# The written order of an MLP's instructions where one unit of columns hands over to the next

## Chip, cores, metric

The kernel runs on one core of a Trainium2 chip. The metric is device time in microseconds (us) of one execution; lower is better. The core has TensorE (PE, with its weight loads PEld), VectorE (DVE), ScalarE (ACT), GpSimd (POOL) and SyncE (SP), which here only issues loads. Each engine works through its own queue in order and waits at an instruction until what it needs is there.

## What is computed

Two decoder layers on 256 tokens of width 2048, in float32. Each layer attends (differential attention in layer 1, dilated windows in layer 2, both with four heads that read a memory), adds the result to the stream x, and ends with the MLP that the change is about:

```python
hm = _rmsnorm(x, g_mlp[i])
x = x + jnp.square(jax.nn.relu(hm @ w_mlp1[i])) @ w_mlp2[i]     # 2048 -> 8192 -> 2048
```

A last RMSNorm follows. In layer 2 the attention needs tables of key distances (`distances`), which are made from an iota.

## The kernel before

**Passes.** A float32 product is made of three fp32r matmuls: each operand is split into `hi` (a copy rounded by ACT) and `lo` (what is left, a subtraction on DVE), and `passes` (L609 to L612) adds hi x hi, hi x lo and lo x hi into one bank of PSUM. `split` (L116 to L118) is that pair of instructions, ACT first, then DVE.

**Units.** The 8192 hidden columns are cut into 8 units of 1024. Unit 0 goes up in the plain way (`up_plain`). Units 1 to 7 go up by a Strassen-like scheme: 8 steps (`step_up`), one for each pair of 128-row slices, each of 7 factors (p1 to p7) of 3 matmuls, 21 in all, which add up in 7 PSUM banks. `prep_up` makes the weights of one step in four parts: loads `b` and `o` (SP) and the sum `s` (DVE, L229); the split of `b` (`bh`, `bl`); `o` from `s` (L233), the split `oh`, a second sum (L235) and the split of `s`; the split of `o` (`th`, `tl`).

**The end of a unit.** `end_up` copies bank p1 (ACT L663), joins the banks on DVE (L666 to L674) into four 128x512 tiles c11, m12, c21 and m22, and squares them on ACT (L615, L616). `to_hT` turns each of these four **blocks** with four transposes on PE (L687) into a PSUM tile `pu` and splits it into `hT` (ACT L117, DVE L118). Blocks 0 and 1 are tokens 0 to 127, blocks 2 and 3 are tokens 128 to 255.

**Down.** Eight groups for each unit (`group_down`): 4 column groups n times 2 halves of tokens t, each of 24 matmuls into a bank `psd`, in the order of four weight pieces k = 0, 2, 4, 6 of two slices each. A piece is a load `raw_d`, a copy `hi_d` (ACT L698, `piece_hi`) and a subtraction `lo_d` (DVE L704, `piece_lo`). ACT then scales the bank into `part` (L723), and POOL issues a DMA that adds it to x (L724).

**Order.** Inside `tc.manual_schedule()` each engine gets its instructions in the order in which the code writes them; outside of it a planner orders them. The written loop runs over the units c and g = 0 to 7: one step of a later unit, then group g (n = g // 2, t = g % 2) of unit c. g = 0 to 6 hold the steps 1 to 7 of unit c + 1, g = 7 holds step 0 of unit c + 2, and `end_up(c + 1)` is written in g = 6 and g = 7. So PE takes 21 matmuls of a step, 24 of a group, and so on, and the weights of the next step and group are made beside them. There are 6 such **passages** from one unit to the next in each layer, 12 in all; the first unit and the last of a layer are written apart.

**Buffers.** PSUM has two tags of four banks: "m" (p1, p2, p5, p7) and "a" (p3, p6, p4 and one bank that `psd` and `pu` use in turn). `hi_d` and `lo_d` have 4 buffers each (WH), so the copy of the next n for piece k waits until PE has read the old piece k. `raw_d` has 3, with the fourth piece (k = 6) in the tag "ux" of `b` and `o` (5 buffers). The joined tiles, the sums of squares (`junk`) and `feat_sum` use the tag "ev" (4), the parts and the temporary tiles the tag "tmp" (6).

Of the kernel before, what the change touches and what calls it, by code (L numbers as in the profile page):

```python
# [17 lines left out]
P = 128  # L18
# [13 lines left out]
EV = 4  # L32
# [26 lines left out]
def trunk(ctx: ExitStack, tc: tile.TileContext, x, mem, g_attn, w_in, w_out, lambda_qk,  # L59
# [292 lines left out]

    def distances(groups, nm):

        dist_i = work.tile([P, 384], I32, tag="tmp", bufs=TMP, name=f"dist_i{nm}")
        nc.gpsimd.iota(dist_i[:, 0:128], pattern=[[-1, 128]], base=0, channel_multiplier=1)
        nc.gpsimd.iota(dist_i[:, 128:384], pattern=[[-1, 256]], base=128, channel_multiplier=1)
        tabs = []
        for gi, (window, dil) in enumerate(groups):
            if gi % 2 == 0:  # L360
                two = upool.tile([P, 2, 384], F32, tag="ut", bufs=UT, name=f"dist{nm}{gi}")
            tab = two[:, gi % 2, :]
            nc.vector.tensor_copy(tab, dist_i)
            keep_if(tab, 0, -1, 1)
            if dil > 1:
                rem_i = work.tile([P, 384], I32, tag="tmp", bufs=TMP, name=f"rem{nm}{gi}")
                nc.vector.tensor_scalar(rem_i, dist_i, dil - 1, None, op0=ALU.bitwise_and)
                rem = work.tile([P, 384], F32, tag="tmp", bufs=TMP, name=f"remf{nm}{gi}")
                nc.vector.tensor_copy(rem, rem_i)
                nc.vector.tensor_scalar(rem, rem, 1.0, FAR, op0=ALU.min, op1=ALU.mult)  # L370
                nc.vector.tensor_tensor(tab, tab, rem, op=ALU.max)
            if window < S:
                keep_if(tab, window, 1, -1)
            tabs.append(tab)
        return tabs
# [66 lines left out]
    for i in range(DEPTH):  # L442
# [156 lines left out]


        NC = DFF // 1024
        hT = [None, None]

        ublk = {}
        final = i == DEPTH - 1
# [52 lines left out]
        def end_up(c):  # L658
# [16 lines left out]
            ublk[c] = ((c11, 0, 0), (m12, 0, 1), (c21, 1, 0), (m22, 1, 1))  # L675
            yield
            squared(c21, c21, 1.0)
            squared(m22, m22, -1.0)

        def to_hT(c):  # L680

            for f in range(2):
                hT[f] = act_tile(f"hT{i}{c}{f}")
            for n, (u, t, f) in enumerate(ublk[c]):
                pt = bank([P, 4, P], f"pu_{i}{c}{n}")
                for k in range(4):
                    nc.tensor.transpose(pt[:, k], u[:, k * P:(k + 1) * P], ident)  # L687
                cols = slice(t * P, (t + 1) * P)
                split(hT[f][:, :, 0, cols], hT[f][:, :, 1, cols], pt)
                yield  # L690

        def piece_hi(c, n, k):
# [21 lines left out]
        def group_down(c, n, t, gemm):  # L714

            ps = bank([P, 512], f"psd{i}{c}{n}{t}", gemm)
            for k in range(8):
                passes(ps, hT[k // 4][:, k % 4, :, t * P:(t + 1) * P], *dw[c, n, k], k == 0, k == 7)
            return ps

        def add_down(c, n, t, ps):
# [33 lines left out]
        next(first)  # L755
        with tc.manual_schedule():
            run(prep_up(1, 0))
            run(first)
            prep = prep_up(1, 1)
            next(prep)  # L760
            step_up(1, 0)
            run(prep)
            piece_hi(0, 0, 0)
            piece_hi(0, 0, 2)
            piece_lo(0, 0, 0)
            turned = None
            for c in range(NC - 1):
                for g in range(8):
                    uc, kp = (c + 1, g + 1) if g < 7 else (c + 2, 0)
# [1 line left out]
                    prep = prep_up(pc, pk) if pc < NC else iter(())  # L771
                    n, t = g // 2, g % 2
                    more = (c, n + 1) if n < 3 else (c + 1, 0)
                    if g == 0:
                        turned = to_hT(c)

                        def turn_first():
                            next(turned)
                            piece_lo(c, 0, 2)
                            next(prep)  # L780

                        def turn_second():
                            next(turned)
                            next(prep)

                        step_up(uc, kp, {1: turn_first, 3: turn_second, 5: lambda: next(turned)})
                        prep_down(c, 0, (1,))
                        run(prep)
                    elif g == 1:
                        step_up(uc, kp, {2: lambda: run(turned)})  # L790
                        run(prep)
                    elif g == 6:
                        step_up(uc, kp)
# [1 line left out]
                        next(ending)  # L795
                        run(prep)
                        next(ending)
                    elif g == 7:
                        if uc < NC:
                            step_up(uc, kp)  # L800
                        for _ in range(3):
                            next(prep, None)
                        run(ending)
                        piece_hi(*more, 0)
                        run(prep)
                        piece_hi(*more, 2)
                        piece_lo(*more, 0)
                    else:
                        step_up(uc, kp)
                        run(prep)  # L810
                    if t == 1 and g < 7:
                        prep_down(*more, (0,))
                    add_down(c, n, t, group_down(c, n, t, False))
                    if t == 1 and g < 7:
                        prep_down(*more, (1,))
            piece_lo(NC - 1, 0, 2)
            prep_down(NC - 1, 0, (1,))
            run(to_hT(NC - 1))
        last_down(NC - 1)
        xT = nxt  # L820

# [9 lines left out]
    def add_last(t, c0, c1, acc):  # L831
# [3 lines left out]
        for f in range(2):  # L835
            for kk in range(4):
                hi, lo = wt[4 * f + kk]
                ah = hT[f][:, kk, 0, t * P:(t + 1) * P]
                al = hT[f][:, kk, 1, t * P:(t + 1) * P]
                for lhs, rhs in ((ah, hi), (ah, lo), (al, hi)):  # L840
                    nc.tensor.matmul(ps[:, c0:c1], lhs, rhs[:, c0:c1], start=n == 0, stop=n == 23)
                    n += 1
# [47 lines left out]
```

## Time and profile before

| | us |
|---|---|
| median of 3 runs | 2244.4 |
| lowest, highest | 2243.36, 2247.9 |
| the profiled execution, its own time | 2243.37 |
| its span in the profile | 2241.6 |
| one passage to the next in the written loop (the copy of piece 4 behind the `part` of g = 5: 583.57, 671.27, 759.01 us) | 87.7 |

TensorE's granted clock, as a share of its full speed, is 0.995 over the span. The MLPs stand at about 500 to 1180 us and 1560 to 2230 us. In the timeline a matmul of 512 columns shows 0.39 us, but one starts about every 0.23 us: they overlap, so lost time on PE is read from the distance of two starts, not from busy time.

### The profile page before, as it was taken

Reading aid. Unit: us, or ns where it says so; the run is one execution under the profiler, and the core shown is the slowest. Engines: PE = TensorE matmul, PEld = TensorE weight load, DVE = VectorE, ACT = ScalarE, POOL = GpSimd, SP = SyncE. Lnnn points to the kernel's source line nnn. Section 1 sums busy time; section 2 is a strip of 40 time slices with the busy share of each in tenths; the row PEclk is TensorE's granted clock in tenths of the full one; section 3 lists DMA queues with packets and bytes.
Section 4 is the critical chain, followed back from the end, with each engine's and each line's share of the span. In section 5 each row is a group of like instructions: output and inputs, shape, how many; then the busy total and the mean of one; then the engine's idle time right before and its main releaser. Section 6 shows DMA issues by size and latency. Waiting matters only on the chain.

```text
span 2241.6 us, 28416 instructions
## 1 busy us (share of the span) xinstructions
PE 2181.0 (97%) x10358; PEld 1794.2 (80%) x10358; DVE 1711.9 (76%) x2084; ACT 1326.3 (59%) x1840; POOL 115.7 (5%) x146
## 2 busy tenths in 40 slices
PE   9999999999999999999999999999999999999998
PEld 7888878887787787877878888888778778777786
DVE  6557766767889888988866665665888989888875
ACT  7445555556666666666655554455666666666664
POOL 0000000000000000000010000000000000000000
PEclk9999999999999999999999999999999999999999
DMA  7665556566677776776745556666677777777674
GB/s 247 189 194 162 152 169 197 170 194 195 203 234 212 205 235 195 228 223 199 215 138 188 160 171 181 194 187 197 193 209 233 206 209 225 207 212 233 195 211 145
DMA packets 262399, 443.50 MB, mean 198 GB/s; under 512 B 14497, under 2 KB 80242, under 8 KB 262002
## 3 DMA queue, kind: packets, MB, share of 16 engines
q1 hardware_dynamic: 245856, 412.14, 58.7%
q0 software_dynamic: 16128, 29.37, 7.3%
q8 instruction: 81, 1.33, 0.2%
q14 instruction: 60, 0.49, 0.1%
q10 hardware_dynamic: 274, 0.17, 0.0%
HBM read 409.12 MB, written 3.15 MB: 184 GB/s over the span
## 4 chain that ended last, share of the span: by engine, by line
PE 81%; ACT 7%; DVE 7%; issue 3%; DMA 1%; ACTq 0%; DVEq 0%; SPq 0%; POOL 0%; POOLq 0%
PE psd L610 8%; PE psd L612 8%; PE psd L611 8%; PE p L610 6%; PE p L611 5%; PE p L612 5%; PE ps_k L145 4%; PE ps_q L145 4%; PE pso L166 2%; PE pso L167 2%; PE pso L165 2%; PE ps_q L141 2%; PE ps_k L141 2%; PE psv L165 2%; PE psv L166 2%
## 5 line engine op out<-in xcount | busy, mean ns | idle before, releaser
L610 PE MATMUL psd<-hi_d,hT 128*128 128x512 f32 x1008 | 394.5, 392 | 3.6 <-ACT hT L117 3.3
L612 PE MATMUL psd<-hi_d,hT 128*128 128x512 f32 x1008 | 392.7, 390 | 2.8 <-DVE hT L118 2.8
L611 PE MATMUL psd<-lo_d,hT 128*128 128x512 f32 x1008 | 392.9, 390 | 0.0
L704 DVE TENSOR_TENSOR lo_d<-raw_d,hi_d 128x1024 fp32r<-128x1024 f32 x252 | 299.1, 1222 | 83.9 <-ACT hi_d L698 83.9
L698 ACT ACTIVATE hi_d<-raw_d 128x1024 fp32r<-128x1024 f32 x252 | 256.5, 1050 | 14.3 <-PE psd L612 8.1
L610 PEld LDWEIGHTS psd<-hi_d,hT 128*128 128x128 f32 x1008 | 189.5, 188 | 49.5 <-DVE hT L118 5.9
L612 PEld LDWEIGHTS psd<-hi_d,hT 128*128 128x128 f32 x1008 | 189.7, 188 | 42.9 <-DVE hT L118 3.6
L117 ACT ACTIVATE th<-o 128x1024 fp32r<-128x1024 f32 x112 | 118.8, 1061 | 174.9 <-DVE o L235 174.1
L611 PEld LDWEIGHTS psd<-lo_d,hT 128*128 128x128 f32 x1008 | 189.8, 188 | 38.8
L118 DVE TENSOR_TENSOR bl<-b,bh 128x1024 fp32r<-128x1024 f32 x112 | 136.5, 1219 | 40.9 <-ACT bh L117 40.9
L724 POOL DMA_DIRECT2D x_sb<-part x112 | 97.5, 871 | 1219.2 <-ACT part L723 1219.2
L117 ACT ACTIVATE sh<-s 128x1024 fp32r<-128x1024 f32 x112 | 118.7, 1060 | 63.7 <-DVE s L229 50.7
L118 DVE TENSOR_TENSOR tl<-o,th 128x1024 fp32r<-128x1024 f32 x112 | 137.3, 1226 | 22.1 <-ACT th L117 16.7
L229 DVE TENSOR_TENSOR s<-b,o 128x1024 f32<-128x1024 f32 x112 | 136.4, 1218 | 4.9 <-DMA o<-in_w_mlp_dram 4.9
L118 DVE TENSOR_TENSOR sl<-s,sh 128x1024 fp32r<-128x1024 f32 x112 | 136.3, 1217 | 0.0
L117 ACT ACTIVATE bh<-b 128x1024 fp32r<-128x1024 f32 x112 | 118.0, 1053 | 13.1 <-PE p L611 12.4
L723 ACT ACTIVATE part<-psd,rsq 128x512 f32<-128x512 f32 x112 | 76.8, 686 | 80.8 <-PE psd L612 79.2
L145 PE MATMUL ps_k<-xT,hi_k 128*128 128x512 f32 x384 | 122.3, 398 | 0.0
L145 PE MATMUL ps_q<-xT,hi_q 128*128 128x512 f32 x384 | 122.0, 399 | 0.0
L118 DVE TENSOR_TENSOR lo_v<-raw_v,hi_v 128x1024 fp32r<-128x1024 f32 x48 | 58.8, 1225 | 50.2 <-ACT hi_v L117 50.1
L610 PE MATMUL p<-bh,cb_xm 128*128 128x512 f32 x224 | 89.7, 400 | 3.9 <-DVE u L670 3.9
L610 PE MATMUL p<-sh,cb_xm 128*128 128x512 f32 x224 | 89.8, 401 | 0.0
(331 smaller groups left out, 4890.8 us busy)
## 6 DMA issues: line engine op xcount, KB each, us to landing
raw_d<-in_w_mlp_dram SPq DMA_DIRECT2D x252, 512.0 KB, 5.8
b<-in_w_mlp_dram SPq DMA_DIRECT2D x112, 512.0 KB, 3.9
o<-in_w_mlp_dram SPq DMA_DIRECT2D x112, 512.0 KB, 3.8
x_sb<-part POOLq DMA_DIRECT2D x112, 256.0 KB, 5.9
raw_q<-in_w_in_dram SPq DMA_DIRECT2D x48, 512.0 KB, 3.8
raw_k<-in_w_in_dram SPq DMA_DIRECT2D x48, 512.0 KB, 3.9
raw_v<-in_w_in_dram SPq DMA_DIRECT2D x48, 512.0 KB, 3.6
raw_o<-in_w_out_dram SPq DMA_DIRECT2D x48, 512.0 KB, 3.7
```

Of the source, the lines that this page charges most:

```text
L117: nc.scalar.activation(dst_hi, src, AF.Copy)
L118: nc.vector.tensor_tensor(dst_lo, src, dst_hi.bitcast(F32), op=ALU.subtract)
L141: nc.tensor.matmul(ps[j][:, 0, :], lo[:, j * P:(j + 1) * P], a[:, 0, :], **f)
L145: nc.tensor.matmul(ps[j].rearrange("p h t -> p (h t)"), hi[:, j * P:(j + 1) * P], a.rearrange("p h t -> p (h t)"), **f)
L165: nc.tensor.matmul(ps[t], ah, hi, start=first and kk == 0, stop=False)
L229: nc.vector.tensor_tensor(s, b, o[:, 0:1].to_broadcast([P, 2, 512]), op=ALU.add)
L610: nc.tensor.matmul(ps, acts[:, 0, :], hi, start=first, stop=False)
L611: nc.tensor.matmul(ps, acts[:, 0, :], lo, start=False, stop=False)
L612: nc.tensor.matmul(ps, acts[:, 1, :], hi, start=False, stop=last)
L698: nc.scalar.activation(hi, raw, AF.Copy)
L704: nc.vector.tensor_tensor(lo, raw, hi.bitcast(F32), op=ALU.subtract)
L724: nc.gpsimd.dma_start(x_sb[:, t, n * 512:(n + 1) * 512], part, accum_op=ALU.add)
```

## The change

- In a passage (g = 0 with c > 0) only blocks 0 and 1 are turned, ahead of the factors at places 2 and 4 of the step; blocks 2 and 3 are turned in the same way in g = 1. Before, three blocks were turned in g = 0 (ahead of places 1, 3 and 5) and one in g = 1.
- The squares of c21 and m22 move from g = 7 into g = 0, between and behind the first two blocks (`ending`).
- At g = 7 the four parts of `prep_up` run without a break; then the copy and the subtraction of piece 0, the group, and only behind the group's `part` the copy of piece 2, whose subtraction is the first of g = 0.
- At g = 1, 3 and 5 the copy of piece 4 is written ahead of the group and of its `part`; behind it come the copy of piece 6 and then the two subtractions.
- First unit: its pieces 0 and 2 are made ahead of the squares of unit 0, and blocks 0 and 1 are turned in step 0 of unit 1 (places 2 and 5), 2 and 3 in g = 1. Before, all four were turned in steps 1 and 2.
- Last unit: blocks 0 and 1 are turned ahead of group g = 7 of the unit before, 2 and 3 behind it; before, all four behind it.
- `dist_i`, the iota from which the distance tables are made, moves from the tag "tmp" to the tag "ev".

```diff
@@ -352,7 +352,7 @@
 
     def distances(groups, nm):
 
-        dist_i = work.tile([P, 384], I32, tag="tmp", bufs=TMP, name=f"dist_i{nm}")
+        dist_i = work.tile([P, 384], I32, tag="ev", bufs=EV, name=f"dist_i{nm}")
         nc.gpsimd.iota(dist_i[:, 0:128], pattern=[[-1, 128]], base=0, channel_multiplier=1)
         nc.gpsimd.iota(dist_i[:, 128:384], pattern=[[-1, 256]], base=128, channel_multiplier=1)
...
@@ -675,18 +675,19 @@
             ublk[c] = ((c11, 0, 0), (m12, 0, 1), (c21, 1, 0), (m22, 1, 1))
             yield
             squared(c21, c21, 1.0)
+            yield
             squared(m22, m22, -1.0)
 
         def to_hT(c):
 
             for f in range(2):
-                hT[f] = act_tile(f"hT{i}{c}{f}")
+                hT[c, f] = act_tile(f"hT{i}{c}{f}")
             for n, (u, t, f) in enumerate(ublk[c]):
                 pt = bank([P, 4, P], f"pu_{i}{c}{n}")
                 for k in range(4):
                     nc.tensor.transpose(pt[:, k], u[:, k * P:(k + 1) * P], ident)
                 cols = slice(t * P, (t + 1) * P)
-                split(hT[f][:, :, 0, cols], hT[f][:, :, 1, cols], pt)
+                split(hT[c, f][:, :, 0, cols], hT[c, f][:, :, 1, cols], pt)
                 yield
 
...
@@ -755,15 +756,12 @@
         next(first)
         with tc.manual_schedule():
             run(prep_up(1, 0))
+            prep_down(0, 0, (0,))
             run(first)
+            turned = to_hT(0)
             prep = prep_up(1, 1)
-            next(prep)
-            step_up(1, 0)
+            step_up(1, 0, {2: lambda: (next(turned), next(prep)), 5: lambda: next(turned)})
             run(prep)
-            piece_hi(0, 0, 0)
-            piece_hi(0, 0, 2)
-            piece_lo(0, 0, 0)
-            turned = None
             for c in range(NC - 1):
                 for g in range(8):
                     uc, kp = (c + 1, g + 1) if g < 7 else (c + 2, 0)
@@ -771,23 +769,29 @@
                     prep = prep_up(pc, pk) if pc < NC else iter(())
                     n, t = g // 2, g % 2
                     more = (c, n + 1) if n < 3 else (c + 1, 0)
-                    if g == 0:
-                        turned = to_hT(c)
-
+                    if g == 0 and c:
                         def turn_first():
                             next(turned)
-                            piece_lo(c, 0, 2)
+                            next(ending)
                             next(prep)
 
                         def turn_second():
                             next(turned)
                             next(prep)
 
-                        step_up(uc, kp, {1: turn_first, 3: turn_second, 5: lambda: next(turned)})
+                        turned = to_hT(c)
+                        piece_lo(c, 0, 2)
+                        step_up(uc, kp, {2: turn_first, 4: turn_second})
+                        prep_down(c, 0, (1,))
+                        next(prep)
+                        run(ending)
+                        run(prep)
+                    elif g == 0:
+                        step_up(uc, kp)
                         prep_down(c, 0, (1,))
                         run(prep)
                     elif g == 1:
-                        step_up(uc, kp, {2: lambda: run(turned)})
+                        step_up(uc, kp, {2: lambda: (next(turned), next(prep)), 4: lambda: run(turned)})
                         run(prep)
                     elif g == 6:
                         step_up(uc, kp)
@@ -795,27 +799,34 @@
                         next(ending)
                         run(prep)
                         next(ending)
+                    elif g == 7 and uc < NC:
+                        step_up(uc, kp)
+                        run(prep)
+                        piece_hi(*more, 0)
+                        piece_lo(*more, 0)
                     elif g == 7:
-                        if uc < NC:
-                            step_up(uc, kp)
-                        for _ in range(3):
-                            next(prep, None)
                         run(ending)
+                        turned = to_hT(c + 1)
+                        next(turned)
+                        next(turned)
                         piece_hi(*more, 0)
-                        run(prep)
-                        piece_hi(*more, 2)
                         piece_lo(*more, 0)
                     else:
                         step_up(uc, kp)
                         run(prep)
                     if t == 1 and g < 7:
                         prep_down(*more, (0,))
+                        piece_hi(*more, 4)
                     add_down(c, n, t, group_down(c, n, t, False))
                     if t == 1 and g < 7:
-                        prep_down(*more, (1,))
+                        piece_hi(*more, 6)
+                        piece_lo(*more, 4)
+                        piece_lo(*more, 6)
+                    elif t == 1:
+                        piece_hi(*more, 2)
+            run(turned)
             piece_lo(NC - 1, 0, 2)
             prep_down(NC - 1, 0, (1,))
-            run(to_hT(NC - 1))
         last_down(NC - 1)
         xT = nxt
```

The other lines rename `hT[f]` to `hT[c, f]`. The number of matmuls, transposes, splits and loads is the same.

## Rows read from the trace of the kernel before

**Rows 1.** The page, part 1: busy time, share of the span and instructions of each engine.

```profile
PE 2181.0 (97%) x10358; PEld 1794.2 (80%) x10358; DVE 1711.9 (76%) x2084; ACT 1326.3 (59%) x1840; POOL 115.7 (5%) x146
```

**Rows 2.** Who PE waited for over the whole span: engine, tile and line that waited, who ended the wait, us in total, times, longest us.

```profile
PE pu L687 <- DVE hT L118: 16.7, 14, 3.4
PE pu L687 <- ACT part L723: 11.3, 12, 1.0
PE p L610 <- DVE u L666: 6.6, 12, 0.6
PE p L610 <- DVE u L670: 3.9, 12, 0.3
PE psd L612 <- DVE hT L118: 2.8, 1, 2.8
```

**Rows 3.** Timeline of PE, the step of g = 7 in one passage of layer 2: start, duration, line, operation, tiles, and in brackets the idle time before it and who ended it.

```profile
1652.53 0.39 PE L610 MATMUL p<-bh,cb_xm 128*128 128x512 f32 x1
...
1653.91 0.47 PE L610 MATMUL p<-oh,cb_xm 128*128 128x512 f32 x1 [0.55 <-DVE u L666]
...
1655.87 0.50 PE L610 MATMUL p<-bh,cb_xm 128*128 128x512 f32 x1 [0.32 <-DVE u L670]
```

**Rows 4.** The same timeline, the step of g = 0 with three turned blocks, up to the first matmul of its group.

```profile
1664.19 0.39 PE L610 MATMUL p<-bh,cb_xm 128*128 128x512 f32 x1
...
1665.97 0.66 PE L687 MATMUL pu<-ident,u 128*128 128x128 f32 x4 [0.94 <-ACT part L723]
1666.38 0.47 PE L610 MATMUL p<-bh,cb_xm 128*128 128x512 f32 x1
...
1668.04 0.66 PE L687 MATMUL pu<-ident,u 128*128 128x128 f32 x4
...
1670.91 0.66 PE L687 MATMUL pu<-ident,u 128*128 128x128 f32 x4 [0.82 <-DVE hT L118]
...
1672.98 0.50 PE L610 MATMUL psd<-hi_d,hT 128*128 128x512 f32 x1
```

**Rows 5.** The same timeline, the step of g = 1 with one turned block, up to the first matmul of its group.

```profile
1678.55 0.39 PE L610 MATMUL p<-bh,cb_xm 128*128 128x512 f32 x1
...
1679.92 0.60 PE L687 MATMUL pu<-ident,u 128*128 128x128 f32 x4
...
1683.81 0.39 PE L610 MATMUL psd<-hi_d,hT 128*128 128x512 f32 x1
```

**Rows 6.** Timeline of DVE from the weights of g = 5 to the joining of the banks (x2 is two instructions in a row).

```profile
1640.04 2.35 DVE L704 TENSOR_TENSOR lo_d<-raw_d,hi_d 128x1024 fp32r<-128x1024 f32 x2
1644.20 2.36 DVE L704 TENSOR_TENSOR lo_d<-raw_d,hi_d 128x1024 fp32r<-128x1024 f32 x2 [1.80 <-ACT hi_d L698]
...
1653.09 0.68 DVE L666 TENSOR_TENSOR u<-t,p 128x512 f32<-128x512 f32 x1
...
1655.12 0.69 DVE L670 TENSOR_TENSOR u<-t,p 128x512 f32<-128x512 f32 x1
```

**Rows 7.** Timeline of ACT: the copies around the `part` of g = 5, and the `part` of g = 7.

```profile
1638.77 2.10 ACT L698 ACTIVATE hi_d<-raw_d 128x1024 fp32r<-128x1024 f32 x2
1642.53 0.69 ACT L723 ACTIVATE part<-psd,rsq 128x512 f32<-128x512 f32 x1 [1.65 <-PE psd L612]
1643.11 2.00 ACT L698 ACTIVATE hi_d<-raw_d 128x1024 fp32r<-128x1024 f32 x2
...
1665.25 0.67 ACT L723 ACTIVATE part<-psd,rsq 128x512 f32<-128x512 f32 x1
```

**Rows 8.** Timeline at the first unit of layer 2: PE from the start of its step 0, through the second turned block, to the first matmul of its first group, and DVE's first split of the weights of step 1.

```profile
1569.42 0.39 PE L612 MATMUL p<-bh,cb_xm 128*128 128x512 f32 x1
...
1579.80 0.92 PE L687 MATMUL pu<-ident,u 128*128 128x128 f32 x4 [3.39 <-DVE hT L118]
...
1585.28 0.50 PE L610 MATMUL psd<-hi_d,hT 128*128 128x512 f32 x1
...
1572.33 1.23 DVE L118 TENSOR_TENSOR bl<-b,bh 128x1024 fp32r<-128x1024 f32 x1 [11.44 <-ACT bh L117]
```

**Rows 9.** Timeline at the last unit: PE in layer 1 (all 16 transposes, then the 14th matmul of the next group), PE in layer 2 (the transposes, then the 8th matmul), and a weight subtraction of DVE in layer 1; then two stretches with length, busy time of PE, PEld, DVE, ACT and POOL (and instructions), PE's granted clock, share of DMA and GB/s.

```profile
1124.70 1.91 PE L687 MATMUL pu<-ident,u 128*128 128x128 f32 x16
...
1136.48 0.40 PE L612 MATMUL psd<-hi_d,hT 128*128 128x512 f32 x1
...
2184.26 1.91 PE L687 MATMUL pu<-ident,u 128*128 128x128 f32 x16
...
2189.95 0.39 PE L612 MATMUL psd<-hi_d,hT 128*128 128x512 f32 x1
...
1127.15 1.66 DVE L704 TENSOR_TENSOR lo_d<-raw_d,hi_d 128x1024 fp32r<-128x1024 f32 x1
...
1128.00:1137.00 9.00, 5.95 (x16) 4.08 (x17) 8.17 (x13) 1.43 (x3) 2.59 (x6) 0.62 0.49 142
2184.00:2194.00 10.00, 8.35 (x43) 6.45 (x42) 6.17 (x8) 4.53 (x7) 0.86 (x1) 1.00 0.74 212
```

**Rows 10.** The loads of the weight pieces over the whole span (KB each, median us from issue to landing), SP's issue of the pieces 0 and 2 for the passage shown above, and who reads the distance tables (times; duration min/median/max in ns; first and last start in us).

```profile
raw_d<-in_w_mlp_dram SPq DMA_DIRECT2D x252, 512.0 KB, 5.8
...
1641.28 1.50 SPq L85 DMA_DIRECT2D raw_d<-in_w_mlp_dram  x2
...
L425 DVE SCALAR_TENSOR_TENSOR e<-dist,sc x36: 545/548/555, 182.9 to 1372.7; 128x384 f32<-128x384 f32 x36
```

More of the change, by code (lines that the diff above doesn't have):

```diff
@@ L601, in trunk @@
         NC = DFF // 1024
-        hT = [None, None]
+        hT = {}
         ublk = {}
@@ L717, in group_down @@
             for k in range(8):
-                passes(ps, hT[k // 4][:, k % 4, :, t * P:(t + 1) * P], *dw[c, n, k], k == 0, k == 7)
+                passes(ps, hT[c, k // 4][:, k % 4, :, t * P:(t + 1) * P], *dw[c, n, k], k == 0, k == 7)
             return ps
@@ L837, in add_last @@
                 hi, lo = wt[4 * f + kk]
-                ah = hT[f][:, kk, 0, t * P:(t + 1) * P]
-                al = hT[f][:, kk, 1, t * P:(t + 1) * P]
+                ah = hT[NC - 1, f][:, kk, 0, t * P:(t + 1) * P]
+                al = hT[NC - 1, f][:, kk, 1, t * P:(t + 1) * P]
                 for lhs, rhs in ((ah, hi), (ah, lo), (al, hi)):
```

## The prediction

> **What bounds the kernel now.** I read busy time first: PE is in work for 2181.0 of 2241.6 us, DVE for 1711.9, ACT for 1326.3 [rows 1]. So only what PE loses can be won. Next, whom PE waited for [rows 2]: four lines come 12 times or more, as often as there are passages. A wait of 0.55 us ends with L666 and one of 0.33 with L670 (6.6/12, 3.9/12), one of 0.94 with a `part` (11.3/12), and 0.82 with an `hT` split (of its 14 times two are 3.39 us long, the rest is about 0.82). Last the timeline of one passage [rows 3 to 5]. From 1655.87 to 1664.19 are 12 matmuls of the step and 24 of the group; less 0.1 us for a slow restart that is 0.228 us each. From 1652.53 to 1683.81, three steps and two groups, are 31.28 us; 111 matmuls at 0.228 are 25.31. A passage thus loses 6.0 us: 1.4 at the two bank waits of g = 7 (1653.91 is 0.70 behind 1652.53 + 3 x 0.228, 1655.87 is 0.59 behind 1653.91 + 6 x 0.228, and 0.1 of restart), 4.0 at the three blocks of g = 0 (8.79 us from 1664.19 to 1672.98 against 4.79), 0.5 at the one block of g = 1 (5.26 against 4.79). The 0.5 is what a block costs that waits for nothing.
>
> **Part by part.** PE's own instructions stay the same; I follow one passage from 1652.53.
>
> *Copy of piece 4 ahead of `part`.* ACT is idle for 1.65 us before the `part` at 1642.53, and DVE then for 1.80 before the subtractions of pieces 4 and 6 [rows 6, 7]. A copy takes 1.05 (2.10 for two). The piece's buffer is free when PE has read the old piece 4, the 18th of 24 matmuls of the group that ends at about 1642.5: six matmuls earlier, 1641.15. So the copy runs 1641.2 to 1642.25 and delays `part` by nothing; behind ACT's queue only that `part` waits, and at worst it is 0.7 late, with `psd`'s bank needed only a step later. DVE goes on at 1642.4; the copy of piece 6 follows `part` (1643.1 to 1644.2) and its subtraction ends at 1645.4 instead of 1646.56. DVE is without a pause from there to L666, so L666 starts 1.14 earlier, at 1651.95, and ends at 1652.65. Factor p2 wants its bank at 1652.53 + 3 x 0.228 = 1653.2: that wait goes. L670 starts at 1653.98, ends at 1654.67; p3 wants it at 1654.58: 0.15 and 0.1 of restart stay. Loss of g = 7: 0.25, and its group starts 1.2 earlier. If the buffers are given out otherwise and the copy starts only when the group ends, `part` is 0.6 late and nothing is won here (loss 1.4).
>
> *g = 7 without squares, copy 2 behind `part`.* Four squares (0.6 each) leave ACT's queue between the weight copies, so `th` follows its sum at once. The group ends at 1663.0, `part` runs 1663.2 to 1663.9 (before: 1665.25), copy 2 to 1664.9, its subtraction, which now heads DVE's queue in g = 0, to 1666.1.
>
> *Blocks 0 and 1.* Place 2 is 6 matmuls after 1663.0, 1664.37, and the bank was freed at 1663.9: the wait of 0.94 goes. Block 0 costs 0.5. Its ACT half can end at 1665.7, but its DVE half stands behind the subtraction of piece 2 and ends at 1666.75. Block 1 wants the bank at 1664.37 + 0.5 + 6 x 0.228 = 1666.25: a new wait of 0.5. Its own cost is 0.5, the group follows at 1669.4. Behind the split DVE holds s (1.22), the other split, bl and the subtractions of pieces 4 and 6, which I find done at 1671.4 and 1672.6; the group needs them at its 14th and 20th matmul, 1672.4 and 1673.7. These margins are about one instruction.
>
> *Blocks 2 and 3.* The group ends at 1674.9; `th` stands before its `part` and ends at 1675.6, `part` at 1676.25, just when place 2 is reached: 0.5. Block 3 wants the bank 1.88 later, and a block frees it in 2.07 (1665.97 to 1668.04, rows 4): 0.2 and 0.5.
>
> *Sum of a passage.* 0.25 + 0.5 + 1.0 + 0.5 + 0.7 = 2.95, against 6.0: 3.0 won, 12 times: 36. Bounds: 1.8 if every block waits half a us more, 3.7 if the waits of p3 and block 1 vanish; 22 to 44.
>
> *First unit.* From 1569.42 to 1585.28 PE does 40 matmuls, 9.1 us: 6.8 lost, 3.39 of it in one wait for block 0's split, which stands behind `th` and two weight copies and subtractions, and 0.5 more for the last block [rows 8]. After: block 0 at 1570.4 and its split behind the squares of unit 0 (end 1571.3); block 1 at 1573.1; both free of waits. But the split of b, at 1572.33 before, now stands behind both blocks: about 1575.6 to 1576.8, where step 1 wants it at 1575.9. I get waits of 1.5 there and 1.0 for the split of s, 2.0 for four blocks, 0.6 of rests: 5.1 against 7.3. 2.2 won in each layer, 4.4; bounds 0 and 8. On SP the pieces 0 and 2 go ahead of step 1's b and o, and 4 and 6 ahead of step 2's; all of them fall into 10 us in which ACT and DVE waited (DVE 11.44), so I cost it at nothing; without that cover it is one landing, 5.8 [rows 10]. In the passages SP's and POOL's orders stay.
>
> *Last unit.* In layer 2 the 8th matmul behind the transposes starts 5.69 after the first transpose; 7 x 0.228 are 1.6: 4.1 lost. After, 8 transposes stand on each side of the group (about 1.0 each), and the subtraction of piece 2 stands behind the splits of blocks 2 and 3, at 2189.1 to 2190.3, with PE at it from 2188.0: 2.3 to 2.4 of waiting, 4.5 lost, 0.4 more than before. In layer 1 the table work stands between: DVE's splits came 2.80 late [rows 2], the granted clock of the stretch was 0.62 where the same stretch of layer 2 had 1.00 [rows 9], that is, part of it lay at 1.2 instead of 2.4 GHz. From 1124.70 to the 14th matmul are 11.78 us, less 13 x 0.228: 8.8. Without the tables it falls to the other layer's 4.5: 4.3 won (bounds 0 and 6).
>
> The Trainium skill (TensorE: Matmul & The Clock Gate, What's actually happening) says that TensorE's half clock is its default and that activity releases it. By that rule the new wait in the last unit could itself bring the half clock; the row of layer 2 with its 1.00 bore a wait of 1.41 without it, and no row shows one of 2.3. By the rule some 2 us more would go in each layer, which is a part of rival (b).
>
> *Tables later.* The tag "ev" hands them on behind the squares that use it in `last_down`, past POOL's last `part` of layer 1, to the start of layer 2's attention; the first reader there stands far behind (the second half of L425's 36). The work is some 5 us of DVE in short pieces where DVE has pauses: nothing, bounds -0.5 and 2.
>
> The Trainium skill (SBUF — State Buffer, Who interferes with whom) says that DVE and GpSimd exclude each other at one port while such instructions run. The row agrees: a subtraction of 1.2 us took 1.66 beside POOL's table work [rows 6, 9]. By the rule the cost moves with the tables to the splits of the attention, 0.5 for each one hit.
>
> *Total.* 36 + 4.4 + 4.3 - 0.4 = 44.3 off 2243.4: 2199.1; the median of the runs is 1.0 above the profiled execution: **2200**. A share of 0.2% (4.5 us) is about what a measurement of this kernel can tell from no change.
>
> **Rivals.** (a) *The one shared bank takes it back.* Each of the four blocks waits for DVE, whose queue in g = 0 has no pause in my reckoning. If block 1 waits 1.2 more and the bank wait of p3 stays whole, a passage wins 1.6: 19, total 27: 2217. For it: DVE is busy in this stretch, and the margins are one instruction. Against: all durations are rows. (b) *The ends win nothing*: the tables aren't later (the planner places them where a buffer of "ev" is free, and block 0 of the last unit now frees one early) the first unit's weights wait, and the clock falls in the last units as it did in layer 1 [rows 9]: 36 alone: 2208. (c) *The load of piece 2 comes onto the path, slower than before.* Its copy now stands alone between `part` and all that DVE does in g = 0. If the load lands later than 1663.9, each us is lost 12 times; from 3.7 late on (44.3/12) the kernel is slower, at 5 us late 2260. For it: nothing stands beside that subtraction as cover. Against: it is issued at 1641.3 to 1642.8 and loads land in 5.8 [rows 10], 15 us before. (d) *The change only moves its waits*: less than 0.2%, 2244.
>
> **How the numbers follow.** Forecast 0.68, (a) 0.13, (b) 0.10, better than the sum (all of the new waits vanish, 2188) 0.02, (c) 0.04, (d) 0.03. Faster: 0.93; same 0.03; slower 0.04. The range holds the forecast with the bounds of the passages that aren't rival (a) (3.6 and 2.3 a passage: 2193, 2208), (b), and (a): 2191 to 2218.
>
> **What would show it.** PE's waits for L666 and for `part` gone from the list of waits; in their place 12 waits of some 0.5 for `hT`, ended by DVE; L666 1.1 us earlier against the step; a passage of 84.7 us instead of 87.7; in the first unit two waits for `bl` and `sl` and no half clock; in layer 1's last unit no table work on DVE. It is wrong if the copies of piece 4 delay `part`, if subtractions 4 and 6 of g = 0 come behind PE, or if the clock falls in the passages.

## The result and the profile after

| | before | after |
|---|---|---|
| median, us | 2245.0 (4 runs, the three above and one more, 2243.36 to 2247.9) | 2196.7 (4 runs, 2195.21 to 2197.5) |
| profiled execution, its own time | 2243.37 | 2197.42 |
| its span | 2241.6 | 2195.6 |
| one passage to the next (block 1's wait in layer 1: 605.87, 690.70, 775.53) | 87.7 | 84.83 |

The ratio is 0.9783 (95% interval 0.9766 to 0.98). The forecast was 2200.0 with 2191 to 2218.

PE has the same instructions as before and nearly the same busy time, in a span 46 us shorter. The page after, busy time by engine (beside [rows 1]):

```profile
PE 2169.9 (99%) x10358; PEld 1791.5 (82%) x10358; DVE 1711.9 (78%) x2084; ACT 1327.4 (60%) x1840; POOL 114.0 (5%) x146
```

Whom PE waited for, after (us in total, times, longest; beside [rows 2]):

```profile
PE pu L688 <- DVE hT L118: 4.7, 12, 0.4
...
PE p L611 <- DVE bl L118: 1.5, 2, 0.8
...
PE p L611 <- DVE sl L118: 1.5, 2, 0.7
...
PE psd L611 <- DVE lo_d L705: 0.6, 2, 0.3
```

The lines for L666 and for `part` are gone. Where the kernel before waited twelve times some 0.82 and twice 3.4 for an `hT` split [rows 2], twelve waits of 0.4 are left, one in each passage, now at block 1. New are two waits each for `bl`, `sl` and `lo_d`, one in each layer. That is the list that the prediction named.

The passage of [rows 3 to 5], 27.25 us earlier here. Timeline of PE: the steps of g = 7, 0 and 1.

```profile
1625.28 0.39 PE L610 MATMUL p<-bh,cb_xm 128*128 128x512 f32 x1
...
1627.49 0.50 PE L610 MATMUL p<-bh,cb_xm 128*128 128x512 f32 x1
...
1635.84 0.39 PE L610 MATMUL p<-bh,cb_xm 128*128 128x512 f32 x1
...
1637.20 0.60 PE L688 MATMUL pu<-ident,u 128*128 128x128 f32 x4
...
1639.59 0.66 PE L688 MATMUL pu<-ident,u 128*128 128x128 f32 x4 [0.40 <-DVE hT L118]
...
1642.15 0.39 PE L610 MATMUL psd<-hi_d,hT 128*128 128x512 f32 x1
...
1647.60 0.39 PE L610 MATMUL p<-bh,cb_xm 128*128 128x512 f32 x1
...
1649.06 0.66 PE L688 MATMUL pu<-ident,u 128*128 128x128 f32 x4
...
1651.13 0.66 PE L688 MATMUL pu<-ident,u 128*128 128x128 f32 x4
...
1653.69 0.39 PE L610 MATMUL psd<-hi_d,hT 128*128 128x512 f32 x1
```

At 0.227 us a matmul the losses are: 0.27 at p3 (1627.49 is 2.21 behind 1625.28, nine matmuls are 2.04; the rest is 0.1 of restart, since the second matmul behind a wait starts about 0.33 and not 0.23 behind the first), 0.43 for block 0, which waits for nothing, 1.06 for block 1 (0.56 of it ahead of its transposes), 0.61 for block 2, 0.70 for block 3. Together 3.1, where the passage before lost 6.0: 2.9 won, 12 times, 34.8.

DVE in the same passage (beside [rows 6]):

```profile
1612.79 3.49 DVE L705 TENSOR_TENSOR lo_d<-raw_d,hi_d 128x1024 fp32r<-128x1024 f32 x3
1616.95 1.23 DVE L705 TENSOR_TENSOR lo_d<-raw_d,hi_d 128x1024 fp32r<-128x1024 f32 x1 [0.67 <-ACT hi_d L699]
...
1624.71 0.68 DVE L666 TENSOR_TENSOR u<-t,p 128x512 f32<-128x512 f32 x1
...
1626.74 0.69 DVE L670 TENSOR_TENSOR u<-t,p 128x512 f32<-128x512 f32 x1
...
1637.70 1.23 DVE L705 TENSOR_TENSOR lo_d<-raw_d,hi_d 128x1024 fp32r<-128x1024 f32 x1 [0.60 <-ACT hi_d L699]
1638.85 0.68 DVE L118 TENSOR_TENSOR hT<-pu,hT 128x512 fp32r<-128x512 f32 x1
```

And ACT (beside [rows 7]):

```profile
1611.52 2.10 ACT L699 ACTIVATE hi_d<-raw_d 128x1024 fp32r<-128x1024 f32 x2
1613.92 1.06 ACT L699 ACTIVATE hi_d<-raw_d 128x1024 fp32r<-128x1024 f32 x1 [0.29 <-PE psd L612]
1615.28 0.69 ACT L724 ACTIVATE part<-psd,rsq 128x512 f32<-128x512 f32 x1 [0.30 <-PE psd L612]
...
1636.04 0.69 ACT L724 ACTIVATE part<-psd,rsq 128x512 f32<-128x512 f32 x1 [0.38 <-PE psd L612]
1636.62 1.05 ACT L699 ACTIVATE hi_d<-raw_d 128x1024 fp32r<-128x1024 f32 x1
```

Read ACT first. The third copy (piece 4) waits 0.29 for PE to be done with the old piece, and ends ahead of the group, so `part` still waits 0.30 for the group and not for ACT. DVE therefore has three subtractions in a row and a pause of 0.67 instead of 1.80. L666 then runs at 1624.71, before PE has even started the step, and only p3 still loses a little. At 1636.04 `part` waits for the end of its group, 0.38; before, it came behind the squares and the copies. The copy of piece 2 follows it with no wait for its load.

The last unit of layer 1, PE (beside [rows 9]):

```profile
1100.81 1.03 PE L688 MATMUL pu<-ident,u 128*128 128x128 f32 x8
...
1111.97 0.50 PE L611 MATMUL psd<-lo_d,hT 128*128 128x512 f32 x1 [0.31 <-DVE lo_d L705]
...
1114.60 0.84 PE L610 MATMUL psd<-hi_d,hT 128*128 128x512 f32 x3
```

Between 1100.81 and 1114.60 lie 49 matmuls, 11.1 us; 2.7 are lost, where the same unit lost 8.8 before. In layer 2 the same rows (2134.25 to 2148.05) lose 2.7 against 4.1. The subtraction of piece 2 makes PE wait 0.31 here. The prediction had 2.3 to 2.4.

### The profile page after: what moved, and what is told of

It reads as the page before. It is cut to its first block, busy times and chain, and to the rows that moved or that the text cites. A ratio compares the mean times of both kernels' runs of the same rounds, so it can differ in the third digit from the quotient of the medians.

```text
span 2195.6 us, 28498 instructions
## 1 busy us (share of the span) xinstructions
PE 2169.9 (99%) x10358; PEld 1791.5 (82%) x10358; DVE 1711.9 (78%) x2084; ACT 1327.4 (60%) x1840; POOL 114.0 (5%) x146
## 4 chain that ended last, share of the span: by engine, by line
PE 94%; ACT 2%; DVE 2%; issue 1%; DMA 1%; SPq 0%; POOL 0%; POOLq 0%; DVEq 0%; ACTq 0%
PE psd L611 10%; PE psd L612 10%; PE psd L610 10%; PE p L610 8%; PE p L611 7%; PE p L612 7%; PE ps_k L145 4%; PE ps_q L145 4%; PE pso L166 3%; PE pso L167 3%; PE pso L165 3%; PE ps_q L141 2%; PE ps_k L141 2%; PE psv L165 2%; PE psv L166 2%; PE psv L167 2%
## 5 line engine op out<-in xcount | busy, mean ns | idle before, releaser
L705 DVE TENSOR_TENSOR lo_d<-raw_d,hi_d 128x1024 fp32r<-128x1024 f32 x252 | 297.4, 1219 | 47.8 <-ACT hi_d L699 47.5
```

The costliest lines, as they stand in the source:

```text
L705: nc.vector.tensor_tensor(lo, raw, hi.bitcast(F32), op=ALU.subtract)
```

## The experiments

All times are medians, in brackets the ratio to the kernel before with its 95% interval; the kernel before was run again beside them (2245.2 to 2245.8). "After" is 2196.7.

### What each part is worth

**e1**, the passages alone: the diffs of e3 and e4 below, and `dist_i` back in the tag "tmp".

> The kernel before with the twelve passages alone changed (two turned blocks a step, copies 2 and 4 and the squares moved); first unit, last unit and tables as before. Theory (the ledger read from the two traces): a passage loses 6.0 us before and 3.1 after, 2.9 x 12 = 34.4, so 2245.0 - 34.4 = 2210.6. Rival 1: the passages are all of it, 2197. Rival 2: the ends and the tables made room for the passages, which alone win half, 2228.

Measured 2210.0, 35.3 less than before (0.9848, 0.9834 to 0.9861). The theory holds; both rivals fall.

**e2**, the tables alone, on the kernel before:

```diff
-        dist_i = work.tile([P, 384], I32, tag="tmp", bufs=TMP, name=f"dist_i{nm}")
+        dist_i = work.tile([P, 384], I32, tag="ev", bufs=EV, name=f"dist_i{nm}")
```

> The kernel before with one line changed: the iota of the distance tables in the tag 'ev'. Theory: the tables leave the last unit of layer 1, whose loss falls from 8.8 to the 4.1 of layer 2: 4.7 less, 2240.3, with no half clock in that stretch. Rival: the planner places the table work where it was, or it hides in either place: 2245. Second rival: the tables cost the opening of layer 2 as much as they leave: 2245 with the last unit's wait gone and new waits in the attention.

Measured 2240.9, 4.3 less (0.9981, 0.9972 to 0.999). Layer 1's last unit, PE, and a stretch with busy times and clock:

```profile
1125.93 1.91 PE L687 MATMUL pu<-ident,u 128*128 128x128 f32 x16
...
1129.25 0.50 PE L610 MATMUL psd<-hi_d,hT 128*128 128x512 f32 x1 [1.41 <-ACT hT L117]
...
1132.98 0.39 PE L612 MATMUL psd<-hi_d,hT 128*128 128x512 f32 x1
```

```profile
1122.00:1132.00 10.00, 8.35 (x44) 6.45 (x43) 6.57 (x8) 8.15 (x12) 1.50 (x2) 1.00 0.78 215
```

The 14th matmul starts 7.05 us behind the first transpose (11.78 before), so 4.1 are lost, as in layer 2, and the granted clock is 1.00 where it was 0.62. One line does all of this; the work itself runs in the attention of layer 2, on DVE at 1180 to 1189 us in this run, and brings no wait for it into PE's list of waits.

**e3**, the changed kernel with the last unit as before:

```diff
                     elif g == 7:
                         run(ending)
-                        turned = to_hT(c + 1)
-                        next(turned)
-                        next(turned)
                         piece_hi(*more, 0)
+                        piece_hi(*more, 2)
                         piece_lo(*more, 0)
...
-                    elif t == 1:
+                    elif t == 1 and uc < NC:
                         piece_hi(*more, 2)
-            run(turned)
             piece_lo(NC - 1, 0, 2)
             prep_down(NC - 1, 0, (1,))
+            run(to_hT(NC - 1))
```

> The changed kernel with the last unit as before: all four blocks turned behind the group, copy of piece 2 ahead of it. Theory (from the traces): the eight early transposes and the planner, which puts matmuls of the other half of the tokens into the wait for piece 2, win 1.4 us in each layer: undone, 2196.7 + 2.8 = 2199.5. Rival (as predicted): the form of before is the better by 0.4 in each layer: 2195.9.

Measured 2199.7, 3.0 more than after (0.9802, 0.9788 to 0.9815). The interval overlaps that of the changed kernel, but the runs don't mix (2198.72 to 2201.48 against 2195.21 to 2197.5). So the new form of the last unit wins about 1.5 in each layer; by the prediction it would have lost 0.4. The same stretch of the last unit in layer 1 and in layer 2 of this run, with length, busy times and granted clock:

```profile
1106.00:1116.00 10.00, 8.35 (x32) 6.17 (x31) 4.76 (x6) 3.53 (x6) 0.86 (x1) 0.83 0.58 183
2143.00:2153.00 10.00, 8.35 (x37) 6.22 (x36) 5.51 (x7) 3.74 (x8) 0.53 (x1) 1.00 0.72 207
```

In both PE waits 1.41 behind its 16 transposes, yet in layer 1 the clock falls and the 14th matmul starts 8.6 us behind the first transpose, in layer 2 it stays and the same takes 7.06, as in e2. So part of what the old form costs is the clock, and not in every execution; without it the new form wins 1.4 (4.1 less 2.7).

**e4**, the changed kernel with the first unit as before:

```diff
-            prep_down(0, 0, (0,))
             run(first)
-            turned = to_hT(0)
             prep = prep_up(1, 1)
-            step_up(1, 0, {2: lambda: (next(turned), next(prep)), 5: lambda: next(turned)})
+            next(prep)
+            step_up(1, 0)
             run(prep)
+            piece_hi(0, 0, 0)
+            piece_hi(0, 0, 2)
+            piece_lo(0, 0, 0)
+            turned = None
```

(and in g = 0 and 1 of c = 0 the blocks at places 1, 3, 5 and 2, as before)

> The changed kernel with the first unit as before: three blocks turned in step 1, one in step 2, the unit's weight pieces behind step 0. Theory: 7.3 us lost in the first unit of each layer against 4.6: 2 x 2.7 = 5.3 more, 2202.0, with the 3.39 us wait for block 0's split back and 11 us without work on DVE. Rival: the wait is hidden in what follows, 2197.

Measured 2201.9, 5.2 more than after (0.9809, 0.9796 to 0.9823). The wait is back: PE's second and third block in layer 2, and two stretches with length, busy times and granted clock.

```profile
1559.16 1.11 PE L688 MATMUL pu<-ident,u 128*128 128x128 f32 x4 [3.40 <-DVE hT L118]
1562.63 1.05 PE L688 MATMUL pu<-ident,u 128*128 128x128 f32 x4
```

```profile
1551.00:1562.00 11.00, 7.61 (x32) 6.05 (x32) 10.20 (x12) 7.24 (x9) 0.00 (x0) 0.82 0.50 144
1562.00:1570.00 8.00, 8.00 (x32) 6.51 (x32) 6.47 (x8) 4.28 (x6) 0.00 (x0) 0.82 0.42 142
```

In the 11 us before, the granted clock was 1.00; here 0.82, so part of both stretches lay at 1.2 instead of 2.4 GHz, and four transposes take 1.05 to 1.11 us instead of 0.60. In the changed kernel the clock is 1.00 from 1535 through 1560.

The four parts sum to 35.3 + 4.3 + 5.2 + 3.0 = 47.8, of the 48.5 between 2245.2 and 2196.7. They add up: if one feeds on another, it is by less than these runs can tell (each interval is some 3 us wide to either side).

### Inside the passage

**e5**, the copy of piece 4 back behind `part`:

```diff
                         prep_down(*more, (0,))
-                        piece_hi(*more, 4)
                     add_down(c, n, t, group_down(c, n, t, False))
                     if t == 1 and g < 7:
-                        piece_hi(*more, 6)
-                        piece_lo(*more, 4)
-                        piece_lo(*more, 6)
+                        prep_down(*more, (1,))
```

> The changed kernel with the copy of piece 4 back behind the group's 'part' at g = 1, 3 and 5. Theory: DVE's 1.8 us pause ahead of the subtractions of pieces 4 and 6 is back, L666 starts 1.1 later against the step, and the bank waits of p2 (0.55) and p3 (0.33) with their restarts come back: 1.4 against 0.27 in a passage, 1.1 x 12 = 13.6 more, 2210. Rival: DVE has the slack elsewhere, and the banks come free for other reasons (no squares in g = 7): 2197.

Measured 2208.6, 11.9 more (0.9833, 0.9818 to 0.9848). PE's waits of this run have the two old lines again:

```profile
PE p L610 <- DVE u L666: 6.6, 12, 0.6
...
PE p L610 <- DVE u L670: 3.8, 12, 0.3
```

**e12**, the same edit alone on the kernel before (the reverse of the diff above):

> The kernel before with one part of the change alone: the copy of piece 4 ahead of the group and its 'part' at g = 1, 3 and 5. Theory: the waits for L666 and L670 fall from 1.4 to 0.3 in a passage, and what follows moves up with them: 12 to 13.6 less, about 2232.5. Rival: the group of g = 7 only ends earlier, 'part' stays late behind the four squares and two copies on ACT, and block 0 waits for the bank that much longer: less than 4 won, 2242.

Measured 2230.7, 14.5 less (0.9937, 0.9923 to 0.995). The wait for `part` is 11.5 us in total as before (11.3): it didn't grow. One copy moved past one `part` is worth 12 to 14.5 of the passages' 35.

**e6**, three blocks in g = 0, all else as changed:

```diff
-                        step_up(uc, kp, {2: turn_first, 4: turn_second})
+                        step_up(uc, kp, {1: turn_first, 3: turn_second, 5: lambda: next(turned)})
```

(and one block, at place 2, in g = 1)

> The changed kernel with three blocks turned in g = 0 (ahead of places 1, 3 and 5) and one in g = 1, all else as changed (copies, squares). Theory: what counts is when the one bank comes free, by 'part' and by DVE's split behind the subtraction of piece 2, not the number of blocks: block 0 waits 0.3, block 1 0.95, block 2 0.3, none in g = 1; 0.5 more in a passage, 2203. Rival: three blocks in one step cost what they cost before, 4.0 and 0.5, against 3.2 now: 1.3 x 12 = 16 more, 2212. Second rival: places are all the same, 2197.

Measured 2205.4, 8.7 more (0.982, 0.9805 to 0.9834), between the theory (2203) and the first rival (2212). The step of g = 0, PE:

```profile
1727.50 0.66 PE L688 MATMUL pu<-ident,u 128*128 128x128 f32 x4 [0.78 <-DVE hT L118]
...
1729.57 0.66 PE L688 MATMUL pu<-ident,u 128*128 128x128 f32 x4
...
1731.65 0.50 PE L610 MATMUL psd<-hi_d,hT 128*128 128x512 f32 x1
```

Block 0 waits 0.26 and block 1 0.93, as the theory has it; what it lacked is the last line. Between 1729.57 and 1731.65 are 2.08 us, and the block with six matmuls takes 1.87: the group too waits 0.2 and a restart for the bank, which the third block holds.

**e7**, squares back in g = 7 and the copy of piece 2 ahead of `part`:

```diff
+                        for _ in range(3):
+                            next(prep)
+                        run(ending)
+                        piece_hi(*more, 0)
                         run(prep)
-                        piece_hi(*more, 0)
+                        piece_hi(*more, 2)
                         piece_lo(*more, 0)
...
-                    elif t == 1:
+                    elif t == 1 and uc == NC:
                         piece_hi(*more, 2)
```

(and the squares taken out of g = 0)

> The changed kernel with the four squares back in g = 7 and the copy of piece 2 back ahead of the group's 'part'. Theory: ACT then reaches 'part' about 1.2 us later (four squares of 0.63 where it paused 1.89, and a copy of 1.05), so block 0 waits 0.8 for the bank and block 1 0.75 for its split behind two subtractions: 1.2 in a passage, 14 more, 2211. Rival: 'part' waits for the end of the group in either order and ACT's pauses take the squares in: 2197.

Measured 2204.0, 7.3 more (0.9811, 0.9795 to 0.9827): the theory's mechanism at half its price. ACT and PE of this run (the step starts at 1724.40):

```profile
1720.28 0.62 ACT L615 ACTIVATE u<-u 128x512 f32<-128x512 f32 x1
...
1725.50 0.66 ACT L724 ACTIVATE part<-psd,rsq 128x512 f32<-128x512 f32 x1
```

```profile
1726.21 0.66 PE L688 MATMUL pu<-ident,u 128*128 128x128 f32 x4 [0.29 <-ACT part L724]
...
1728.83 0.66 PE L688 MATMUL pu<-ident,u 128*128 128x128 f32 x4 [0.57 <-DVE hT L118]
```

`part` starts 1.10 behind the step's start, not 0.20 as in the changed kernel: 0.9 late, since the squares began as soon as ACT was free and partly filled its pause. Block 0 waits 0.29, block 1 0.57.

**e8**, the subtraction of piece 2 behind block 0's split:

```diff
                             next(turned)
+                            piece_lo(c, 0, 2)
                             next(ending)
...
                         turned = to_hT(c)
-                        piece_lo(c, 0, 2)
```

> The changed kernel with the subtraction of piece 2 written behind block 0's split instead of ahead of it. Theory: block 1's new wait (0.40 in a passage) is the split's place in DVE's queue; it goes, and piece 2 is ready 1.9 us ahead of its use: 4.8 less, 2192. Rival: DVE is full through this stretch, and the wait comes back at the subtractions of pieces 4 and 6 or at block 1's split in the group: 2197.

Measured 2197.5 (0.9783, 0.9769 to 0.9798): no gain, the rival is right. PE's second block and group in g = 0, and DVE:

```profile
1723.60 0.66 PE L688 MATMUL pu<-ident,u 128*128 128x128 f32 x4
...
1726.46 0.50 PE L610 MATMUL psd<-hi_d,hT 128*128 128x512 f32 x1
```

```profile
1723.46 1.22 DVE L705 TENSOR_TENSOR lo_d<-raw_d,hi_d 128x1024 fp32r<-128x1024 f32 x1
1724.59 1.22 DVE L229 TENSOR_TENSOR s<-b,o 128x1024 f32<-128x1024 f32 x1
1725.72 0.69 DVE L118 TENSOR_TENSOR hT<-pu,hT 128x512 fp32r<-128x512 f32 x1
```

Block 1's wait is down to 0.19, the time that a block needs in the bank. But its split now stands behind a subtraction and a sum, ends at 1726.41, and the group's first matmul starts at 1726.46, 0.4 late: `psd` needs the bank that block 1 holds.

**e9**, e8 with the sum `s` behind block 1's split as well (the `next(prep)` of `turn_first` goes behind the pieces 4 and 6):

> The changed kernel with the subtraction of piece 2 behind block 0's split, as in the run before, and the sum s of the next weights behind block 1's split too. Theory: the group's first matmul needs the bank that block 1 holds, so what counts is when DVE has done both splits; with only a subtraction between them block 1 waits 0.19 (the time of a block in the bank) and the group nothing: 0.37 less in a passage, 4.4 in all, 2192.3. Rival: DVE's work is all needed at its time, and the wait comes back at the subtractions of pieces 4 and 6 or at the next step's weights: 2197.

Measured 2201.5, 4.8 more than after (0.9806, 0.9793 to 0.982). In g = 0 it does what the theory says: block 1 0.19, the group nothing. Then the rival, in a place that nobody had named: the sum is 1.2 later, and with it the copies `oh`, `sh` and `th`. ACT, and block 2 of g = 1:

```profile
1734.86 1.06 ACT L117 ACTIVATE th<-o 128x1024 fp32r<-128x1024 f32 x1 [1.79 <-DVE o L235]
1735.83 0.67 ACT L724 ACTIVATE part<-psd,rsq 128x512 f32<-128x512 f32 x1
```

```profile
1736.55 0.66 PE L688 MATMUL pu<-ident,u 128*128 128x128 f32 x4 [0.73 <-ACT part L724]
```

`th` waits 1.79 for its sum with `part` behind it, and block 2 waits 0.73 for the bank that `part` reads.

**e10**, e9 with blocks 7 matmuls apart, inside a factor, and p6 ahead of p5 and p7 in a unit's last step:

```diff
-                step_up(uc, kp, {2: turn_first, 4: turn_second})
+                step_up(uc, kp, {6: turn_first, 13: turn_second})
...
+            if kp == KP - 1:
+                order = ("p1", "p3", "p2", "p6", "p5", "p7", "p4")
```

(the places are counted in matmuls here; in g = 1 they are 7 and 14)

> The run e9 with two more edits: the blocks stand 7 matmuls apart instead of 6 (inside a factor), and in the last step of a unit factor p6 comes ahead of p5 and p7, so that L667 (0.59 of waiting for p6) and L670 come earlier. Theory: block 1 and block 3 wait 0.2 less each, block 2 0.1, and the 0.27 at p3 goes: 0.75 in a passage, 9 more than e9 wins, 2183.5. Rival 1: a split inside a factor costs as much as it saves, only p3's 0.27 is won, 3: 2189. Rival 2: neither, 2192.

Measured 2196.4 (0.9782, 0.9768 to 0.9795), 5.2 less than e9. The waits of blocks 1 and 3 go (0.2 each, 12 times, 4.8) and a turned block inside a factor costs no more than one between two. The 0.27 at p3 stays: in the passages DVE's L666 to L670 follow each other without a pause behind the splits of the weights, so an earlier p6 is worth nothing. The 0.59 of waiting that I had read stands only in the last unit. What e9 brought stays too, at block 2 of g = 1:

```profile
1733.04 0.66 PE L692 MATMUL pu<-ident,u 128*128 128x128 f32 x4 [0.76 <-ACT part L728]
```

Over the span PE waits 9.1 us for `part` here (8.7 in e9, no such line in the changed kernel).

**e11**, e10 with the first unit changed:

```diff
+            next(prep)
-            step_up(1, 0, {6: lambda: (next(turned), next(prep)), 15: lambda: next(turned)})
+            step_up(1, 0, {6: lambda: next(turned), 15: lambda: (next(prep), next(turned))})
```

> The run e10 with the first unit's order changed as well: the loads and the sum of step 1's weights are written ahead of step 0, the split of b ahead of block 1. Theory: the waits for bh, bl and sl (0.25, 0.77 and 0.73 in each layer) go: 3.5 less than e10. Rival: the split of b must wait for its buffer, which PE frees late in step 0, and delays block 1's split and the group instead: no less than e10.

Measured 2192.4 (0.9768, 0.9755 to 0.9782), 3.9 less than e10: the waits for `bh` and `bl` are gone, that for `sl` (0.8 in each layer) is not. From the last matmul of unit 0 to the first of the second group are 22.5 us in each layer, 24.0 in e10, so 3.0 of the 3.9 lie there. It is the fastest version here, about 4 us under the changed kernel; its five runs (2191.61 to 2194.62) all lie under the four of that (2195.21 to 2197.5), though the intervals of the ratios overlap. Left open: e11 without e9's late sum, or with `th` behind `part` in g = 0, was not run, and PE waits 9.1 us for `part` in e11 as in e10.

## Why the prediction was right, and where it was off

**The passage** carried it: 36 forecast, 35.3 in e1. Its steps can be laid beside the rows, less the shift of 27.25. Copy of piece 4 at 1613.95, measured 1613.92; L666 at 1624.70, measured 1624.71; L670 at 1626.73, measured 1626.74; `part` at 1635.95, measured 1636.04; losses 0.25, 0.5, 1.0, 0.5 and 0.7 against 0.27, 0.43, 1.06, 0.61 and 0.70. The reason is that the work on every queue was known with its duration, so only the order had to be followed. e5 and e12 show the largest step by itself, e7 and e6 the two others. PE's clock didn't fall in the passages, which the prediction had named as a sign of being wrong: it is 1.00 from 60 to 2180 us.

**Rival (a)** was near: the margins on DVE are one instruction, and e9 shows that one sum a place later gives back more than it wins. It failed since in the order as written only block 1's split is late by more than 0.2. **Rival (c)**: the copy of piece 2 follows `part` with no wait for its load; the load doesn't come onto the path. **Rival (b)** fell with e2, e3 and e4, each a gain of its own (e3's is the smallest).

**Last unit: the step that was off.** "The subtraction of piece 2 stands behind the splits of blocks 2 and 3 ... 2.3 to 2.4 of waiting, 4.5 lost, 0.4 more than before." Measured: 0.31 of waiting, 2.7 lost, 1.4 less than before in layer 2 (e3: 1.5 in each). I had PE wait in the order of the code, but `last_down` lies outside the written order. PE's order as built has the other half of the tokens in the gap (names shortened; 9737 is the bank of t = 0, 9763 that of t = 1):

```
L610 MATMUL psd_9737<-hi_d_9706,hT_9654
L610 MATMUL psd_9763<-hi_d_9672,hT_9654
... (6 more of psd_9763)
L611 MATMUL psd_9737<-lo_d_9722,hT_9654
```

Seven matmuls of group t = 1, which need no more than piece 0 and the copy of piece 2, fill the time until the subtraction is there: 1.6 us of the 2.3. The subtraction itself came when the prediction had it: in layer 2 PE would have stood at it from 2143.07 to 2145.41, 2.3 us. The splits of blocks 2 and 3, which t = 1 needs, had just been made.

**Tables** in layer 1's last unit: the reason was right: with the table work gone the unit looks like that of layer 2. That the forecast of 4.3 and e2's 4.3 are the same is in part luck: the forecast had the new form's 4.5 in it, and the tables alone are 8.8 less 4.1, 4.7, by the rows. At the new place, in the changed kernel, a subtraction beside POOL's table work took 1.21 us (at 1160.05), where one had taken 1.66 at the old [rows 9]; what stretched was POOL's own instruction at 1160.07, 1.45 against 0.51. At the old place POOL's were stretched too (1.60 at 1127.68). By the Trainium skill (SBUF — State Buffer, Who interferes with whom), which the prediction weighed, DVE and GpSimd exclude each other at a port: these durations fit that, with GpSimd as the one that waits at 1160.

**First unit**: 4.4 forecast, 5.2 in e4; by the rows 6.0 (from the last matmul of unit 0 to the first of the second group 27.74 and 26.90 us before, 24.33 in both layers after). Block 0's split no longer stands behind weight work [rows 8], and both early blocks wait for nothing; the waits that take its place, for `bl` and `sl`, are 0.77 and 0.73 and a restart each, where 1.5 and 1.0 were reckoned:

```profile
1551.65 0.50 PE L611 MATMUL p<-bl,cb_xm 128*128 128x512 f32 x1 [0.77 <-DVE bl L118]
...
1554.72 0.50 PE L611 MATMUL p<-sl,cb_xm 128*128 128x512 f32 x1 [0.73 <-DVE sl L118]
```

Part of the gain is the clock, 0.82 in e4 behind the wait of 3.40. The Trainium skill (TensorE: Matmul & The Clock Gate, What's actually happening) has the half clock as the default that activity releases; this row agrees. What it would do with the wait of 2.3 that the prediction had in the last unit stays open, since PE didn't wait: the clock there was 1.00 (1109 to 1118). The prediction read from layer 2 of the kernel before that a wait of 1.41 leaves the clock alone; e3 has the same wait with a clock of 0.83, so that row was no safe ground.

**The rest**: 46.0 off the span, and the ledger has 34.8 + 6.0 + 6.1 + 1.4 = 48.3; against it stands what lies ahead of the first MLP. The last matmul of unit 0 in layer 1 is at 508.80 us before and at 510.81 after. In the profiles of the other kernels it is anywhere from 507.82 to 512.46; two waits in the first 100 us (PE for the load of x and for `hi_km`) make up much of that, up to 1.4 and 0.4 to 1.9 us long. The new tag does reach this stretch, since layer 1 makes distance tables as well: its iota moves from 1.3 to 14.4 us. No wait of PE for the tables comes of it, and the three kernels with the old tag (508.80 to 509.99) lie among those with the new one.

## What to carry to other kernels

When one engine is at 97% and everything else has slack, write the queues out as lists with durations and ask of each instruction that another engine waits for: what stands ahead of it that could stand behind? One copy ahead of one `part` won 12 to 14.5 us of 2245. Count every user of a shared bank, the next group too: moving the work that delays one user behind it moved the wait to the next (e8, e9). And find out which stretches a planner orders: there a wait that you reckon in the order of the code may be filled with other work.

## What the runs showed of the hardware

A wait of 3.4 us on PE was followed by a lower granted clock: in e4 0.82 over the next 8 us, four transposes in 1.05 instead of 0.60 us, matmuls 0.43 us apart (1560.50, 1560.93) instead of 0.23. All five kernels with the old first unit (before, e1, e2, e4, e12) have this wait in both layers, and each time the clock is 0.74 to 0.84 over the 10 to 13 us around it. So such a wait costs more than its length. A wait of 1.41 behind 16 transposes went either way: in the last unit of the old form, without table work, the clock fell in two of seven cases (0.83 in layer 1 of e3 and in layer 2 of e1) and stayed at 1.00 in the others. The new form of the last unit shows no such fall in any of its nine kernels. A turned block ahead of the second or third matmul of a factor cost PE no more than one between two factors (0.45 in e10, 0.44 in e9).
